# Gathering the second expert table in 2 KB half rows, into buffers of their own

## The chip, the core and the metric

The kernel runs on one NeuronCore of a Trainium2 chip. The metric is the device time of one execution in microseconds (us). The engines named are TensorE (PE, with its weight loads as PEld), VectorE (DVE), ScalarE (ACT), GpSimd (POOL), which issues the indirect transfers, and SyncE (SP), which issues all the others. Sixteen DMA engines move the data of both queues.

## The reference

One decoder layer for 1024 prompt tokens and 8 sample tokens: three mixers (a state-space scan, a convolution, attention to a memory) fed by one projection, then a PEER feed-forward, in which every token picks 128 of 16384 experts (8 heads, 16 each). All in float32.

```
x <- LN1(ALPHA * x + W_out( g_A * SSD(x) + g_B * ConformerConv(x) + g_C * MemCrossAttn(x) ))
x <- LN2(ALPHA * x + PEER(x))
# PEER for a block of tokens t (nt, 1024):
idx, gate = top-16 routing per head            # (nt, 8, 16)
u = jnp.take(u_tab, idx, axis=0)               # rows of 1024 floats
act = gelu(einsum('td,thkd->thk', t, u))
v = jnp.take(v_tab, idx, axis=0)
return einsum('thk,thkd->td', gate * act, v)
```

The first table is `peer_u`, the second `peer_v`; a row of either is 4 KB.

## The kernel before

The prompt is cut into three groups of 256, 384 and 384 tokens. For each group `main` runs the mixers as a long list of 128-column weight products on PE. The PEER layer of groups 0 and 1 (2 and 3 blocks of 128 tokens) is done by gathering rows, in the shadow of the products of the groups behind them. The PEER layer of the last group is done densely in `dense_group`: a loop over 128 chunks of 128 experts, with one product with the first table (24 matmuls, L200), a multiplication by the gate (`weigh`, L1353 on DVE), splits into high and low parts (L176, L191 on DVE) and 18 matmuls with the second table (L1385) in each.

A block goes through two stages:

- `block_u` (L447): 128 indirect transfers, each bringing one 4 KB row of the first table to each of 128 partitions (512 KB in all); DVE multiplies and sums each (L455).
- `block_v` (L480): the same with the second table. While `strips` is true the sum over experts is done on PE: for each of 32 values of m four gathers are made, and `four` (L489) multiplies them, eight matmuls together (L501; two column halves times four row strips). When the last group's mixers near their end `strips` becomes false, and the last two blocks go through `block_v2` and `second_table` on DVE instead: one scalar-tensor-tensor of 128x1024 for each gather (L544). `sample_experts` does the same for the 8 sample tokens with 64-row gathers.

All gathers are issued by POOL, one after another, at one line (L442). All rows of both tables, and the accumulators and layer-norm tiles of this part, share one pool of eight 4 KB buffers named `uv` (`UVB = 8`).

The order of the work is made at build time. Before each product `spread` (L271) adds a pace to two counters (one for each table) and takes that many steps of the tables' generators; a step is one gather. `PHASES` and `PACE` hold the paces. What has to follow a gather with a delay (`four`) is put into `late` with a number of steps (`VLAG`). A scheduler then lays the instructions of each engine in a fixed order; each engine works through its own in that order. So a step that is late holds whatever stands behind it on the same engine.

Of the kernel before, what the change touches and what calls it, by code (L numbers as in the profile page):

```python
# [8 lines left out]
F32 = mybir.dt.float32  # L9
# [9 lines left out]
P = 128  # L19
# [10 lines left out]
EPS = 1e-5  # L30
NEG = -3.0e38
TAPS = 31
UVB = 8
TICKS = (4, 6, 5)
PTICK = (1, 1, 0)

PHASES = tuple(dict(zip(("ssd", "out0", "out1", "att", "merge", "rest"), x)) for x in (
    ((0, 0),) * 6,
    ((1.7, 2), (1.8, 1.8), (1.8, 1.8), (2.2, 1.8), (1.4, 1.8), (2.4, 1.8)),
    ((1.4, 2), (1.8, 1.8), (1.8, 1.8), (2.2, 1.8), (1.4, 1.8), (2.4, 1.8))))  # L40
PACE = (1.5, 2.0), (1.0, 1.0), (2.2, 2.2)
LAG = 4
# [2 lines left out]
PRE = 6  # L45
EARLY = 30
STEP = 4
VLAG = 6
TLAG = 10
E2B = 7  # L50
BLKB = 28
# [17 lines left out]
def hybrid_layer(ctx: ExitStack, tc, I, O):  # L69
# [16 lines left out]
    def blk(n=N, dt=F32):  # L86
        t = blkp.tile([P, NW], dt, name="b")
        return t[:, :n]
# [358 lines left out]
    def block_u(g, c, idx, gate):  # L447

        x1 = pep.tile([P, D], F32, name="x1", bufs=1)
        sp.dma_start(x1, x1d[g][c])  # L450
        av = pep.tile([P, P], F32, name="av", bufs=3)
        for s in range(P):
            u = pep.tile([P, D], F32, name="uv", bufs=UVB)
            gather(u, I["peer_u"], idx[:, c, s:s + 1])
            dve.scalar_tensor_tensor(u, u, 1.0, x1, op0=OP.mult, op1=OP.mult, accum_out=av[:, s:s + 1])  # L455
            yield
        act.activation(av, av, AF.Gelu)
        dve.tensor_tensor(av, av, gate[:, c], op=OP.mult)

        def turned():  # L460

            if not strips[0]:
                tables[1].append(block_v(g, c, idx, av, None, None))
                return
            ix = blk(P)
            act.activation(ix, idx[:, c], AF.Copy)
            pt = pst()
            pe.transpose(pt[:, 0:P], av, ident)
            pe.transpose(pt[:, P:2 * P], ix, ident)
            avt = pep.tile([P, P], F32, name="avt", bufs=2)  # L470
            act.activation(avt, pt[:, 0:P], AF.Copy)
            ixt = pep.tile([P, P], I32, name="ixt", bufs=2)
            dve.tensor_copy(ixt, pt[:, P:2 * P])
            tables[1].append(block_v(g, c, idx, av, avt, ixt))

        while len(tables[1]) > 1:
            yield
        late.append([TLAG, turned])

    def block_v(g, c, idx, av, avt, ixt):  # L480


        if not strips[0]:
            yield from block_v2(g, c, idx, av)
            return
        active.append(1)
        va = []

        def four(m, vs):  # L489
            if m == 0:  # L490
                va.extend(pva() for _ in range(2))
            w = slide[m % 2]
            act.activation(w[:, :, 31], avt[:, m:P:32], AF.Copy)

            before = None
            for dh in range(2):
                for j in (3, 0, 1, 2):
                    with ExitStack() as order:
                        if before is not None:
                            order.enter_context(tc.issue_after(before))  # L500
                        before = pe.matmul(va[dh][32 * j:32 * j + 32], w[:, j, 31 - m:63 - m],  # L501
                                           vs[j][:, dh * 512:dh * 512 + 512], start=(m == 0), stop=(m == 31)).ins

        for m in range(32):
            vs = []
            for j in range(4):
                v = pep.tile([P, D], F32, name="uv", bufs=UVB)
                gather(v, I["peer_v"], ixt[:, 32 * j + m:32 * j + m + 1])
                vs.append(v)
                if j < 3:  # L510
                    yield
            late.append([VLAG, lambda m=m, vs=vs: four(m, vs)])
            yield
        done = []
        late.append([VLAG, lambda: done.append(1)])
        while not done:
            yield
        xr = pep.tile([P, D], F32, name="uv", bufs=UVB)
        sp.dma_start(xr, x1d[g][c])
        for dh in range(2):  # L520
            hs = slice(dh * 512, dh * 512 + 512)
            dve.scalar_tensor_tensor(xr[:, hs], xr[:, hs], ALPHA, va[dh], op0=OP.mult, op1=OP.add)  # L522
        active.pop()
        layer_norm2(xr, P, pep.tile([P, D], F32, name="uv", bufs=UVB))
        sp.dma_start(O[f"yp{g}"][c], xr)

    def block_v2(g, c, idx, av):

        acc = pep.tile([P, D], F32, name="uv", bufs=UVB)
        yield from second_table(P, P, idx[:, c], av, acc)  # L530
        xr = pep.tile([P, D], F32, name="uv", bufs=UVB)
        sp.dma_start(xr, x1d[g][c])
        dve.scalar_tensor_tensor(xr, xr, ALPHA, acc, op0=OP.mult, op1=OP.add)
        layer_norm2(xr, P, acc)
        sp.dma_start(O[f"yp{g}"][c], xr)
# [119 lines left out]
    def main(G):  # L655
# [41 lines left out]
        for half in range(2):  # L697
            us = []
            phase("ssd")
            for q in (2 * half, 2 * half + 1):  # L700
                us += ssd_group(G, q, G.pre if q == 0 else ssd_front(G, q))
                if ms is None:
                    ms = rp.tile([P, N], F32, name="ms")[:, :nt]
                sums(q)
                sq = [blk(nt) for _ in range(4)]
                for x, u in zip(sq, us[-4:]):
                    act.activation(x, u, AF.Square)
                squares.append((q, sq))
            if half == 0:
                acc_o = [accp.tile([P, NW], F32, name="acc")[:, :no] for _ in range(8)]  # L710
                acc = [x[:, :nt] for x in acc_o]
            if last and half == 0:
                drain()
            ops = pack(G, us, (C_NW, 8 * half), S["u"][:, 8 * half:8 * half + 8] if last else None)
            phase("out0" if half == 0 else "out1")
            if g == RIDE and half == 1:
                side.append(samples())
            for f in range(8):
                ps = out_product(G, I["wso"][half * 8 + f], ops, f, "ba", half == 1)
                if f == 0:  # L720
                    sums(4)
                    if half == 1:
                        rs = rstd_of(ms, 2048, blk(nt))
                if half == 0:
                    act.activation(acc[f], ps, AF.Copy)
                else:
                    dve.tensor_tensor(acc[f], acc[f], ps, op=OP.add)
                    dve.tensor_tensor(acc[f], acc[f], rs, op=OP.mult)
                    pg = proj(64 + f, G)
                    sg = blk(nt)  # L730
                    act.activation(sg, pg, AF.Sigmoid)
                    dve.tensor_tensor(acc[f], acc[f], sg, op=OP.mult)
                if f % 4 == 3:
                    conv_block(2 * half + f // 4)
# [783 lines left out]
```

## Time and profile before

| | |
|---|---|
| median of 3 runs | 4560.6 us (4558.73 to 4568.82) |
| profiled execution | 4556.38 us, its span 4554.6 us |
| mean granted TensorE clock | 0.936 of full speed |
| PE / DVE / ACT / POOL busy, share of the span | 86% / 72% / 38% / 35% |
| indirect transfers by POOL | 640 first table, 640 second table, 32 for the samples |

Four parts of the span matter. Until 852 us nothing is gathered. From there to about 1400 us only the first table is gathered. From 1412 to 3426 us the three strip blocks run beside the products (gaps at 1975 to 2099 and 2640 to 2762 us). From 3431 us the dense loop runs, with the gathers of the last two blocks and of the samples beside it, until 4482 us; PE's last matmul of the loop is at 4513 us. In the rows below, busy times are in us, `x` counts instructions, `L` is a line of the kernel before.

### The profile page before, as it was taken

How to read it: one execution, taken by the hardware profiler on the slowest of the kernel's cores; microseconds unless marked ns; L12 is line 12 of the kernel's file. 1: busy time of each engine (PE TensorE's matmuls, PEld its weight loads, DVE VectorE, ACT ScalarE, POOL GpSimd, SP SyncE). 2: the span in 40 equal slices, each digit the busy share in tenths (PEclk: the TensorE clock that was granted, in tenths of full speed). 3: DMA queues.
4: the chain of work that ended last, by engine and by line, in shares of the span. 5: the costliest groups of instructions: out<-in, count | busy, mean ns of one | idle time of the engine just before them, and what ended most of it. 6: DMA issues, size and time to landing. Idle time of an engine off the chain costs nothing. (4 is left out here: it accounts for less than half of the span.)

```text
span 4554.6 us, 58299 instructions
## 1 busy us (share of the span) xinstructions
PE 3933.1 (86%) x19901; PEld 3047.6 (67%) x19901; DVE 3289.7 (72%) x7235; ACT 1751.8 (38%) x3696; POOL 1593.4 (35%) x1316
## 2 busy tenths in 40 slices
PE   8998899688898788975888888888996999889996
PEld 8888788567675455553665665445664788778895
DVE  4458835869698546675766796458996899888876
ACT  5475525346432204342362332113562333333333
POOL 0000000123333554413444536534322566556631
PEclk9999999899899998987999999999997999999998
DMA  5435555556677898835878879978879999999985
GB/s 176 149 124 171 180 164 169 202 205 226 220 241 245 302 343 311 291 139 178 282 282 321 304 260 337 341 236 282 305 283 312 359 382 393 343 317 304 389 280 188
DMA packets 410043, 1199.42 MB, mean 263 GB/s; under 512 B 42465, under 2 KB 111713, under 8 KB 407569
## 3 DMA queue, kind: packets, MB, share of 16 engines
q0 software_dynamic: 186880, 679.56, 42.2%
q1 hardware_dynamic: 222864, 516.13, 32.8%
q8 instruction: 157, 2.57, 0.2%
q14 instruction: 142, 1.16, 0.1%
HBM read 1141.59 MB, written 53.93 MB: 262 GB/s over the span
## 5 line engine op out<-in xcount | busy, mean ns | idle before, releaser
L442 POOL DMA_INDIRECT uv<-in_peer_u,idx x640 | 759.0, 1186 | 1831.9 <-DVE idx L422 852.1
L200 PE MATMUL mm<-xt,wh 128*128 128x384 f32 (+1 forms) x4224 | 1045.5, 333 | 37.5 <-ACT b L923 23.9
L455 DVE SCALAR_TENSOR_TENSOR uv<-uv,x 128x1024 f32<-128x1024 f32 x640 | 775.7, 1220 | 395.0 <-DMA uv<-in_peer_u,idx 347.1
L200 PEld LDWEIGHTS mm<-xt,wh 128*128 128x128 f32 x4224 | 745.3, 193 | 100.3 <-issue 33.1
L211 PE MATMUL mm<-b,wr 128*128 128x256 f32 (+2 forms) x2304 | 724.9, 467 | 60.9 <-ACT b L739 34.1
L200 PE MATMUL mm<-xt,wl 128*128 128x384 f32 (+1 forms) x2112 | 692.0, 328 | 37.7 <-DVE wl L191 37.5
L189 ACT ACTIVATE wh<-wr 128x1024 fp32r<-128x1024 f32 x362 | 382.9, 1058 | 864.4 <-PE mm L200 327.0
L442 POOL DMA_INDIRECT uv<-in_peer_v,ixt x384 | 427.6, 1113 | 688.1 <-PE va L501 205.5
L211 PEld LDWEIGHTS mm<-b,wr 128*128 128x128 f32 x2304 | 438.4, 196 | 310.3 <-issue 45.4
L191 DVE TENSOR_TENSOR wl<-wr,wh 128x1024 fp32r<-128x1024 f32 x362 | 441.9, 1221 | 247.1 <-ACT wh L189 229.6
L442 POOL DMA_INDIRECT uv<-in_peer_v,idx x256 | 348.2, 1360 | 345.0 <-DVE uv L544 194.2
L200 PEld LDWEIGHTS mm<-xt,wl 128*128 128x128 f32 x2112 | 406.9, 193 | 57.6 <-DVE wl L191 43.4
L678 DVE SCALAR_TENSOR_TENSOR b<-raw,cc,b 128x384 f32<-128x384 f32 (+1 forms) x720 | 408.7, 569 | 9.9 <-ACT b L676 3.4
L544 DVE SCALAR_TENSOR_TENSOR uv<-uv,av 128x1024 f32<-128x1024 f32 (+1 forms) x269 | 343.5, 1280 | 12.9 <-DMA uv<-in_peer_v,idx 9.9
L501 PE MATMUL va<-uv,slide 128*32 128x512 f32 x1536 | 228.2, 714 | 133.3 <-DMA uv<-in_peer_v,ixt 133.3
L501 PEld LDWEIGHTS va<-uv,slide 128*32 128x32 f32 x1536 | 45.0, 120 | 244.4 <-DMA uv<-in_peer_v,ixt 148.6
L200 PE MATMUL st<-b,wh 128*128 128x384 f32 x784 | 205.7, 344 | 0.5 <-ACT b L832 0.5
L200 PE MATMUL tp<-b,wh 128*128 128x384 f32 x784 | 204.5, 342 | 0.0
L164 ACT ACTIVATE b<-acc 128x384 fp32r<-128x384 f32 x128 | 66.8, 525 | 348.4 <-PE va L1385 261.7
L176 DVE TENSOR_TENSOR wl<-e,wh 128x512 fp32r<-128x512 f32 x256 | 165.1, 684 | 24.2 <-ACT wh L164 22.1
L1385 PE MATMUL mm<-wh,b 128*128 128x512 f32 x512 | 165.2, 404 | 13.7 <-ACT b L164 10.1
L1385 PE MATMUL va<-wh,b 128*128 128x512 f32 x512 | 164.5, 403 | 10.9 <-DVE uv L522 10.9
(409 smaller groups left out, 6382.8 us busy)
## 6 DMA issues: line engine op xcount, KB each, us to landing
wr<-in_win SPq DMA_DIRECT2D x264, 512.0 KB
wr<-in_peer_ut SPq DMA_DIRECT2D x128, 512.0 KB
e<-in_peer_v SPq DMA_DIRECT2D x256, 256.0 KB
wr<-in_wso SPq DMA_DIRECT2D x48, 512.0 KB
wr<-in_wq SPq DMA_DIRECT2D x48, 512.0 KB
gd<-xt SPq DMA_DIRECT2D x16, 1536.0 KB
xt<-gd SPq DMA_DIRECT2D x16, 1536.0 KB
wr<-in_wmo SPq DMA_DIRECT2D x24, 512.0 KB
```

What stands on the lines that cost most here:

```text
L164: act.activation(hi, src, AF.Copy)
L176: dve.tensor_tensor(l, src, f32(h), op=OP.subtract)
L189: act.activation(wh, wr, AF.Copy)
L191: dve.tensor_tensor(wl, wr, f32(wh), op=OP.subtract)
L200: pe.matmul(ps, a[:, k], b[k0 + k], start=(i == 0), stop=(i == n - 1))
L211: pe.matmul(ps, w[:, k], xs[k], start=(k == 0), stop=(k == 7))
L442: pool.indirect_dma_start(out=dst, out_offset=None, in_=table, in_offset=bass.IndirectOffsetOnAxis(ap=idx_col, axis=0))
L455: dve.scalar_tensor_tensor(u, u, 1.0, x1, op0=OP.mult, op1=OP.mult, accum_out=av[:, s:s + 1])
L501: before = pe.matmul(va[dh][32 * j:32 * j + 32], w[:, j, 31 - m:63 - m], vs[j][:, dh * 512:dh * 512 + 512], start=(m == 0), stop=(m == 31) ...
L544: dve.scalar_tensor_tensor(acc, v, av[:, s:s + 1], acc, op0=OP.mult, op1=OP.add)
L678: dve.scalar_tensor_tensor(cv, raw[:, i:i + nt], col(C_FW, j * TAPS + i), cv, op0=OP.mult, op1=OP.add)
L1385: pe.matmul(outs[2 * tbk + dh], a[:, ts], v[:, dh * 512:dh * 512 + 512], start=(c == 0 and i == 0), stop=(c == P - 1 and i == 2))
```

## The change

Second-table rows are no longer gathered as 4 KB rows into the shared pool. The table is seen as 32768 rows of 2 KB, and two gathers, with indices 2i and 2i+1, bring the two halves. They land in eight 2 KB buffers of their own (`vv`); the shared pool `uv` keeps four 4 KB buffers. The memory is the same. A step of the second table's generator is now two half gathers; `four` is called for each half with four matmuls and waits `VLAG = 4` steps instead of 6. `block_v2` does two 128x512 instructions for each expert. The pace of the first table in group 1's `ssd` phase goes from 1.7 to 2.3. The indices are computed once for each block (`halves`, two DVE instructions), and `ms` moves from the pool `rp` to the block pool. The sample tokens still use `second_table` and `uv`.

```diff
-UVB = 8
+UVB = 4
+VB = 8
-    ((1.7, 2), (1.8, 1.8), (1.8, 1.8), (2.2, 1.8), (1.4, 1.8), (2.4, 1.8)),
+    ((2.3, 2), (1.8, 1.8), (1.8, 1.8), (2.2, 1.8), (1.4, 1.8), (2.4, 1.8)),
-VLAG = 6
+VLAG = 4
...
+        def halves(src):
+            h = pep.tile([P, 2, P], I32, name="half", bufs=2)
+            for dh in range(2):
+                dve.tensor_scalar(h[:, dh], src, 2.0, float(dh), op0=OP.mult, op1=OP.add)
+            return h
...
-            ixt = pep.tile([P, P], I32, name="ixt", bufs=2)
-            dve.tensor_copy(ixt, pt[:, P:2 * P])
-            tables[1].append(block_v(g, c, idx, av, avt, ixt))
+            tables[1].append(block_v(g, c, av, avt, halves(pt[:, P:2 * P])))
...
+    vhalf = I["peer_v"].rearrange("e (h d) -> (e h) d", h=2)
+    def half_row(idx_col):
+        v = pep.tile([P, 512], F32, name="vv", bufs=VB)
+        gather(v, vhalf, idx_col)
+        return v
...
-            for dh in range(2):
-                for j in (3, 0, 1, 2):
-                        before = pe.matmul(va[dh][32 * j:32 * j + 32], w[:, j, 31 - m:63 - m],
-                                           vs[j][:, dh * 512:dh * 512 + 512], start=(m == 0), stop=(m == 31)).ins
+            for j in (3, 0, 1, 2):
+                    before = pe.matmul(va[dh][32 * j:32 * j + 32], w[:, j, 31 - m:63 - m], vs[j],
+                                       start=(m == 0), stop=(m == 31)).ins
+        for m in range(32):
+            for dh in range(2):
-            vs = []
-            for j in range(4):
-                v = pep.tile([P, D], F32, name="uv", bufs=UVB)
-                gather(v, I["peer_v"], ixt[:, 32 * j + m:32 * j + m + 1])
-                vs.append(v)
-                if j < 3:
-                    yield
-            late.append([VLAG, lambda m=m, vs=vs: four(m, vs)])
-            yield
+                vs = []
+                for j in range(4):
+                    vs.append(half_row(ixh[:, dh, 32 * j + m:32 * j + m + 1]))
+                    if j == 1:
+                        yield
+                late.append([VLAG, lambda m=m, dh=dh, vs=vs: four(m, dh, vs)])
+                yield
...
-        yield from second_table(P, P, idx[:, c], av, acc)
+        for s in range(P):
+            for dh in range(2):
+                a = acc[:, dh * 512:dh * 512 + 512]
+                v = half_row(ixh[:, dh, s:s + 1])
+                if s == 0:
+                    dve.tensor_scalar(a, v, av[:, 0:1], None, op0=OP.mult)
+                else:
+                    dve.scalar_tensor_tensor(a, v, av[:, s:s + 1], a, op0=OP.mult, op1=OP.add)
+            yield
```

Three places show how the order moves. First POOL in the middle of the dense loop, before (`uv` filled from `peer_u` is the first table, from `peer_v` the second) and now (`vv` is a half row):

```order
L442 DMA uv_29115<-in_peer_u,idx1_16049 128x1024
L442 DMA uv_29118<-in_peer_v,idx1_16049 128x1024
L442 DMA uv_29121<-in_peer_u,idx1_16049 128x1024
L442 DMA uv_29124<-in_peer_v,idx1_16049 128x1024
L442 DMA uv_29127<-in_peer_u,idx1_16049 128x1024
L442 DMA uv_29196<-in_peer_v,idx1_16049 128x1024
```

```order
L443 DMA uv_28985<-in_peer_u,idx1_16438 128x1024
L443 DMA vv_28991<-in_peer_v,half_25912 128x512
L443 DMA vv_28997<-in_peer_v,half_25912 128x512
L443 DMA uv_28994<-in_peer_u,idx1_16438 128x1024
L443 DMA vv_29000<-in_peer_v,half_25912 128x512
L443 DMA vv_29006<-in_peer_v,half_25912 128x512
L443 DMA uv_29003<-in_peer_u,idx1_16438 128x1024
L443 DMA vv_29009<-in_peer_v,half_25912 128x512
L443 DMA vv_29081<-in_peer_v,half_25912 128x512
```

Where one gather of each table stood, there are now one and two: three instructions for the same rows.

Second, DVE over one chunk of the dense loop (`wl` and `b` are the low parts that PE waits for, `acc` is the weighed activation), before and now:

```order
L544 SCALAR_TENSOR_TENSOR uv<-uv,av 128x1024
L1353 TENSOR_TENSOR acc<-acc,xt 128x384
L191 TENSOR_TENSOR wl<-wr,wh 128x1024
L455 SCALAR_TENSOR_TENSOR uv,av<-uv,x_24769 128x1024
L544 SCALAR_TENSOR_TENSOR uv<-uv,av 128x1024
L176 TENSOR_TENSOR wl<-e_29720,wh 128x512
L176 TENSOR_TENSOR wl<-e_29724,wh 128x512
L544 SCALAR_TENSOR_TENSOR uv<-uv,av 128x1024
L455 SCALAR_TENSOR_TENSOR uv,av<-uv,x_24769 128x1024 x2
L191 TENSOR_TENSOR wl<-wr,wh 128x1024
```

```order
L549 SCALAR_TENSOR_TENSOR uv<-vv,av,uv 128x512 x2
L1373 TENSOR_TENSOR acc<-acc,xt 128x384
L192 TENSOR_TENSOR wl<-wr,wh 128x1024
L549 SCALAR_TENSOR_TENSOR uv<-vv,av,uv 128x512 x2
L456 SCALAR_TENSOR_TENSOR uv,av<-uv,x_25537 128x1024
L177 TENSOR_TENSOR wl<-e_30845,wh 128x512
L177 TENSOR_TENSOR wl<-e_30849,wh 128x512
L549 SCALAR_TENSOR_TENSOR uv<-vv,av,uv 128x512
L456 SCALAR_TENSOR_TENSOR uv,av<-uv,x_25537 128x1024
L549 SCALAR_TENSOR_TENSOR uv<-vv,av,uv 128x512 x3
L192 TENSOR_TENSOR wl<-wr,wh 128x1024
```

The rows of a gather stand between the low parts as before, at the same pace for each chunk; each second-table row is two instructions of half the width.

Third, PE at one set of the first strip block (`va` is the accumulator in PSUM, `slide` the weights), before and now:

```order
L200 MATMUL mm<-xt,wh 128x384 x2
L200 MATMUL mm<-xt,wl 128x384
L501 MATMUL va<-uv,slide_133 32x512 x8
L200 MATMUL mm<-xt,wh 128x384 x2
L200 MATMUL mm<-xt,wl 128x384
```

```order
L201 MATMUL mm<-xt,wl 128x384
L514 MATMUL va<-vv,slide_134 32x512 x4
L212 MATMUL mm<-b,wr 128x384 x8
L514 MATMUL va<-vv,slide_134 32x512 x4
L201 MATMUL mm<-xt,wh 128x384 x2
```

Eight matmuls that stood together are now two sets of four with a product between them.

## Rows read from the trace of the kernel before

**Rows 1.** The page: busy time by engine, and DMA share in 40 slices.

```profile
PE 3933.1 (86%) x19901; PEld 3047.6 (67%) x19901; DVE 3289.7 (72%) x7235; ACT 1751.8 (38%) x3696; POOL 1593.4 (35%) x1316
DMA  5435555556677898835878879978879999999985
```

**Rows 2.** Stretches (from:to, us): strip blocks 0, 1, 2, then four of the dense loop.

```profile
core 0: us, PE busy (x) PEld busy (x) DVE busy (x) ACT busy (x) POOL busy (x), PEclk, DMA share, GB/s
1412.00:1975.00 563.00, 483.23 (x2204) 311.48 (x2205) 342.37 (x825) 154.87 (x335) 259.77 (x238) 0.93 0.83 298
2099.00:2640.00 541.00, 461.31 (x2318) 322.29 (x2319) 355.05 (x623) 204.76 (x525) 266.62 (x234) 0.92 0.83 295
2762.00:3426.00 664.00, 576.34 (x2665) 350.26 (x2661) 487.18 (x1603) 234.86 (x324) 273.12 (x242) 0.95 0.82 298
...
3590.00:4072.00 482.00, 442.28 (x2120) 393.53 (x2119) 422.65 (x580) 158.28 (x266) 283.51 (x212) 0.95 1.00 364
4072.00:4222.00 150.00, 139.57 (x679) 123.01 (x677) 130.26 (x156) 55.81 (x90) 103.34 (x67) 0.99 1.02 310
4222.00:4361.00 139.00, 134.86 (x662) 121.35 (x663) 120.02 (x135) 48.73 (x80) 77.56 (x54) 0.98 0.99 366
4361.00:4486.00 125.00, 125.00 (x628) 113.10 (x628) 91.51 (x110) 45.90 (x76) 44.31 (x33) 1.00 0.80 268
```

**Rows 3.** PE's and POOL's longest waits on gathers: total us, times, longest.

```profile
PE va L501 <- DMA uv<-in_peer_v,ixt: 133.3, 45, 10.8
...
POOL uv L442 <- DVE uv L455: 783.2, 262, 38.8
POOL uv L442 <- PE va L501: 344.4, 75, 27.2
```

**Rows 4.** Chain of waits in strip block 2: start us, us, what.

```profile
2821.62 7.68 DMA uv<-in_peer_v,ixt
...
2829.35 3.47 PE va L501 x16
...
2839.11 7.56 DMA uv<-in_peer_v,ixt
```

**Rows 5.** Line L442, the gathers: ns min/median/max, first and last start us.

```profile
L442 POOL DMA_INDIRECT uv<-in_peer_u,idx x640: 932/1067/2877, 852.6 to 4019.1; - x160
L442 POOL DMA_INDIRECT uv<-in_peer_v,ixt x384: 932/938/2813, 1396.8 to 3417.4; - x192
L442 POOL DMA_INDIRECT uv<-in_peer_v,idx x256: 932/1296/4541, 3431.1 to 4482.5; - x128
L442 POOL DMA_INDIRECT uv<-in_peer_u,s_idx x16: 893/1400/7182, 4022.9 to 4114.8; - x16
```

**Rows 6.** Timeline in the dense loop, DVE and POOL: start us, us, [idle before <-releaser].

```profile
3594.74 1.21 DVE L455 SCALAR_TENSOR_TENSOR uv<-uv,x 128x1024 f32<-128x1024 f32 x1
3595.09 1.68 POOL L442 DMA_INDIRECT uv<-in_peer_u,idx  x1 [0.65 <-DVE uv L544]
...
3597.07 0.94 POOL L442 DMA_INDIRECT uv<-in_peer_v,idx  x1 [0.30 <-issue]
3597.08 0.57 DVE L1353 TENSOR_TENSOR acc<-acc,xt 128x384 f32<-128x384 f32 x1
...
4249.90 1.86 POOL L442 DMA_INDIRECT uv<-in_peer_v,idx  x1 [5.63 <-DVE uv L544]
```

**Rows 7.** DVE groups by shape: busy us, mean ns of one, idle before.

```profile
L544 DVE SCALAR_TENSOR_TENSOR uv<-uv,av 128x1024 f32<-128x1024 f32 x254 | 325.2, 1280 | 11.6 <-DMA uv<-in_peer_v,idx 9.9
L176 DVE TENSOR_TENSOR wl<-e,wh 128x512 fp32r<-128x512 f32 x256 | 165.1, 684 | 24.2 <-ACT wh L164 22.1 <-ACT b L832 2.0
L678 DVE SCALAR_TENSOR_TENSOR b<-raw,cc,b 128x384 f32<-128x384 f32 x480 | 293.7, 615 | 7.1 <-ACT b L676 1.8
```

**Rows 8.** DMA queues: packets, MB, time as a share of 16 engines.

```profile
q0 software_dynamic: 186880, 679.56, 42.2%
q1 hardware_dynamic: 222864, 516.13, 32.8%
```

More of the change, by code (lines that the diff above doesn't have):

```diff
@@ L458, in block_u @@
         dve.tensor_tensor(av, av, gate[:, c], op=OP.mult)
+        def halves(src):
[3 more added lines that the diff above has]
+            return h
         def turned():
             if not strips[0]:
-                tables[1].append(block_v(g, c, idx, av, None, None))
+                tables[1].append(block_v(g, c, av, None, halves(idx[:, c])))
                 return
@@ L478, in block_u, with block_v @@
         late.append([TLAG, turned])
-    def block_v(g, c, idx, av, avt, ixt):
+    vhalf = I["peer_v"].rearrange("e (h d) -> (e h) d", h=2)
[3 more added lines that the diff above has]
+        return v
+    def block_v(g, c, av, avt, ixh):
         if not strips[0]:
-            yield from block_v2(g, c, idx, av)
+            yield from block_v2(g, c, av, ixh)
             return
@@ L487, in block_v, with four @@
         va = []
-        def four(m, vs):
-            if m == 0:
+        def four(m, dh, vs):
+            if m + dh == 0:
                 va.extend(pva() for _ in range(2))
             w = slide[m % 2]
-            act.activation(w[:, :, 31], avt[:, m:P:32], AF.Copy)
+            if dh == 0:
+                act.activation(w[:, :, 31], avt[:, m:P:32], AF.Copy)
             before = None
-            for dh in range(2):
-                for j in (3, 0, 1, 2):
-                    with ExitStack() as order:
-                        if before is not None:
-                            order.enter_context(tc.issue_after(before))
-                        before = pe.matmul(va[dh][32 * j:32 * j + 32], w[:, j, 31 - m:63 - m],
-                                           vs[j][:, dh * 512:dh * 512 + 512], start=(m == 0), stop=(m == 31)).ins
-        for m in range(32):
-            vs = []
-            for j in range(4):
-                v = pep.tile([P, D], F32, name="uv", bufs=UVB)
-                gather(v, I["peer_v"], ixt[:, 32 * j + m:32 * j + m + 1])
-                vs.append(v)
-                if j < 3:
-                    yield
-            late.append([VLAG, lambda m=m, vs=vs: four(m, vs)])
-            yield
+            for j in (3, 0, 1, 2):
+                with ExitStack() as order:
+                    if before is not None:
+                        order.enter_context(tc.issue_after(before))
+                    before = pe.matmul(va[dh][32 * j:32 * j + 32], w[:, j, 31 - m:63 - m], vs[j],
+                                       start=(m == 0), stop=(m == 31)).ins
+        for m in range(32):
+            for dh in range(2):
+                vs = []
[5 more added lines that the diff above has]
+                yield
         done = []
@@ L525, in block_v, with block_v2 @@
         sp.dma_start(O[f"yp{g}"][c], xr)
-    def block_v2(g, c, idx, av):
+    def block_v2(g, c, av, ixh):
         acc = pep.tile([P, D], F32, name="uv", bufs=UVB)
-        yield from second_table(P, P, idx[:, c], av, acc)
+        for s in range(P):
[7 more added lines that the diff above has]
+            yield
         xr = pep.tile([P, D], F32, name="uv", bufs=UVB)
@@ L702, in main @@
                 if ms is None:
-                    ms = rp.tile([P, N], F32, name="ms")[:, :nt]
+                    ms = blk(nt)
                 sums(q)
```

## Prediction

> **What bounds the kernel now.** I read the page first, then the stretches, then the waits of PE and POOL, then the chain inside a stretch, and last the rows of the gathers. The page shows PE busy 86% of the span and no other engine above 72% [rows 1], so at first sight PE's program sets the time and POOL, at 35%, has room. The DMA digits climb to 8 and 9 in the second half. An average over stages hides what counts here, so the stretches come next [rows 2].
>
> In the three strip blocks PE is busy 86%, 85% and 87%, DVE 61% to 73%, POOL 41% to 49%, DMA 82% to 83%. The largest wait of PE is that of `four` for its second-table rows: 133.3 us in 45 pieces [rows 3]. The chain shows how that comes about [rows 4]: a gather of the second table (7.68 us until its data are used), the matmuls of `four`, and then, from 2839 us, the next such gather (7.56 us). POOL waited 344 us in all for those matmuls and 783 us for DVE's first-table rows [rows 3], since both kinds of row share eight buffers. So a strip set (four rows; 563 us / 31 = 18 us in block 0) is a loop of buffer, gather and matmul that is a little longer than PE's own work.
>
> In the dense loop DMA is at 0.99 to 1.02 from 3590 to 4361 us, DVE at 86% to 88%, PE at 92% to 97%; from 4361 us on PE is never idle [rows 2]. The cuts at 3590, 4072, 4222, 4361 and 4486 us are where DVE weighs chunks 30, 80, 96, 112 and 127, so that the order of either kernel can be counted against them.
>
> **POOL: twice the instructions for the second table.** This is the term that decides. A gather is issued one at a time; its shortest time is 932 ns for 128 rows and 893 ns for 64 rows [rows 5], so neither half the rows nor half the bytes helps much, and I take a half-row gather at the time of a whole one (the row of 64 as the lower end is 4% below). Between two gathers that wait for nothing lie 0.30 us [rows 6]. The floor is then 0.94 + 0.30 = 1.24 us for each gather. It is not reached in general: 3595.09 took 1.68 us, and at its start a DVE instruction with two SBUF inputs had 0.86 us left (3594.74 + 1.21); 3597.07 took 0.94 us, and the DVE instruction beside it began just behind it [rows 6]. A gather looks as if it waits for the two-input DVE instruction that runs when it starts. Such an instruction of 128x1024 takes 1.28 us; halves of 512 should take about 0.70 us each, between 0.615 for 384 columns and 0.684 for another operation on 512, rounded up for the in-place accumulator [rows 7]. Halves therefore hold a gather for less time.
>
> The Trainium skill speaks against such a hold ("SBUF — State Buffer", Who interferes with whom): an instruction with two SBUF inputs blocks only those GpSimd instructions that read SBUF, and writing descriptors is inferred to be spared. The pair of rows just read disagrees, so the sum follows the rows; what the page's rule would give is rival C.
>
> The mean time of a gather with its gap, from the stretches [rows 2]: 3590 to 4072 283.51/212 + 0.30 = 1.64 us; 4072 to 4222 103.34/67 + 0.30 = 1.84 us; 4222 to 4361 77.56/54 + 0.30 = 1.74 us. The upper end is a gather that is always held: 1.68 + 0.30 = 1.98 us beside both kinds of row, 1.86 + 0.30 = 2.16 us beside second-table rows alone [rows 6].
>
> Dense loop. DVE's order ties the rows to the chunks: `acc` and `wl`, for which PE waits, stand behind the rows of the chunk before, so a late gather holds DVE and then PE. What POOL must issue between the cuts, counted in the changed order, against the time of the stretch now:
>
> - chunks 30 to 80: 103 first-table gathers and 205 halves, 308 x 1.64 = 505 us against 482: +23. Floor 382 us, no loss; upper end 610 us, +128.
> - chunks 80 to 96: 1 + 55 halves + 30 for the samples, 86 x 1.84 = 158 us against 150: +8. Floor 107, no loss; upper end 86 x 2.0 = 172, +22. The samples' rows now have two free `uv` buffers at a time, which is in this upper end.
> - chunks 96 to 112, where the order packs the second table densest: 118 halves + 2, 120 gathers. Here I take 1.55 us, below 1.74, since all row instructions are halves: 186 us against 139: +47. Floor 149, +10; upper end 259, +120.
> - chunks 112 to 127: 74 halves, 115 us against 125: nothing, as PE covers it. Upper end 160, +35.
>
> Together +78 us, with +10 and +305 as the ends. Before chunk 30 the 55 gathers fit (90 us in the 159 from the first at 3431 us [rows 5]), and the 20 halves behind chunk 127 lie beside the matmuls of the last chunks.
>
> **DVE.** 256 instructions of 1.28 us become 512 of about 0.70: 256 x 0.12 = +31 us, 12 of them in chunks 30 to 80. DVE there goes from 423 to 435 us, below POOL's 505, so POOL hides it. Without that cover it would cost up to 31. The index instructions are two for each of five blocks: nothing.
>
> **DMA.** The gather queue moved 679.56 MB in 42.2 points of busy share (16.10 MB for each), the other queue, with smaller packets, 15.74 MB [rows 8]. At the latter rate the 335.5 MB of the second table cost 0.5 points more, 22 us of the span, some 9 of them in the dense loop. The slower pace there hides them; if POOL were not the bound they would show. The lower end is no gain: the bytes are the same.
>
> **Strips.** What goes: second-table rows no longer wait for a buffer that a first-table row holds, each half set is used and freed by itself, and the loop of [rows 4] becomes two loops that overlap. PE could get back up to the 133 us of [rows 3]. What comes: 31 sets of four more gathers in each block. Block 0: (238 + 124) x (259.77/238 + 0.30 = 1.39) = 503 us of 563; block 1: 358 x 1.44 = 516 of 541; block 2: 366 x 1.43 = 523 of 664 [rows 2]. POOL is then busy or in its gap 89%, 95% and 79% of the time, in order, with first-table rows queued behind second-table rows whose buffers are not free and the reverse. The next late thing behind the buffer is POOL's own queue, about as long as the loop it replaces. I take 0; the ends are -133 (no wait left) and, at the dense loop's 1.64 us, 594, 587 and 600 us: +31 +46 + 0 = +77. The waits I cannot see are those on the four `uv` buffers of the first table: DVE, not PE, meets them first, and DVE has a quarter of the time free there.
>
> The higher pace in group 1's `ssd` phase moves first-table gathers forward into a stretch where only the first table is gathered; nothing.
>
> **Sum.** 4556.4 (the profiled execution; span 4554.6) + 78 + 0 = 4634 us. The median of the runs shown is 4 us above that execution: 4638, say 4640 us.
>
> **Rivals.**
> A, the decoupling wins: the strips lose their 133 us of waits, and the dense loop costs only what POOL's floor and DVE make of it (+10 to +78). 4560 - 133 + 60 = about 4490 us. For it: the wait is the largest of PE, and POOL fits on average in all three blocks. Against it: 95% of an in-order queue in block 1. It decides if at least 85 us of the 133 go.
> B, POOL binds in both: the strips at +77 and the dense loop midway to its upper end (78 to 305: +190) give 4560 + 267 = about 4825 us. For it: the gathers of 1.68 and 1.86 us. Against it: half rows hold POOL for less.
> C, no hold by two-input instructions: POOL at 1.24 us everywhere, dense +10, strips with POOL far from full, perhaps half the 133 back, DVE's and DMA's 31 + 9 no longer hidden: 4560 + 10 + 40 - 66 = about 4545 us. (By that page's rule; the trace disagrees, as said.)
>
> **Chances.** Forecast 0.57 (own range 4585 to 4720), A 0.22, B 0.13, C 0.08. A measurement of this kernel tells 0.2%, 9 us, from no change. Faster: A and most of C, 0.27; same: 0.06, from the low edge of the forecast and the rest of C; slower: 0.67. The range leaves the lower half of A and the upper half of B out: 4490 to 4800.
>
> **What would show it.** POOL's count of gathers goes to 1952 and its busy share from 35% to over 50%. Right: in the dense loop POOL rests almost only in 0.30 us gaps, DVE's idle time is put down to half rows, the stretch from chunk 96 to 112 grows most (139 to over 170 us), and chunk 112 to the end stays. The strip blocks last within 30 us of now, with PE waiting for half rows. The gather beside half-width DVE rows is shorter than 1.86 us. Wrong: POOL still idle for a third of the dense loop, or strip blocks shorter by 30 us each.

## The result and the profile after

| | before | changed |
|---|---|---|
| median (4 runs each) | 4559.7 us (4552.5 to 4568.8) | 4909.2 us (4902.6 to 4918.7) |
| profiled execution's span | 4554.6 us | 4900.7 us |
| granted TensorE clock, mean | 0.936 | 0.915 |
| PE / DVE / POOL busy | 86% / 72% / 35% | 83% / 68% / 48% |

The changed kernel takes 1.076 times as long [1.0735, 1.0785]. The prediction was 4640 us with a range up to 4800: the sign was right, the size was not, by 269 us.

The page of the changed kernel, for [rows 1]:

```profile
PE 4054.2 (83%) x19901; PEld 3097.9 (63%) x19901; DVE 3328.5 (68%) x7498; ACT 1745.7 (36%) x3695; POOL 2333.1 (48%) x1956
DMA  5445554667678886628678678788879999988885
```

Of the 346 us of span, 121 are PE's own busy time (4054.2 against 3933.1 for the same 19901 matmuls, at the lower granted clock) and 225 its idle time. POOL is still only at 48%, which says as little as its 35% did before.

The place of the loss is read by the same cuts as [rows 2]: DVE weighs chunk 30 at 3798 us (3590 before), and chunks 80, 96, 112 and 127 at 4311, 4499, 4690 and 4821 us. The stretches of the changed kernel between them (from:to, length, busy us of each engine and its instructions, clock, DMA share, GB/s):

```profile
3798.00:4311.00 513.00, 453.11 (x2113) 397.01 (x2113) 424.71 (x666) 158.04 (x266) 402.58 (x312) 0.94 0.96 337
4311.00:4499.00 188.00, 150.95 (x688) 131.57 (x687) 133.06 (x191) 55.91 (x91) 134.33 (x88) 0.93 0.80 244
4499.00:4690.00 191.00, 154.05 (x672) 135.59 (x671) 135.10 (x201) 48.17 (x80) 149.98 (x118) 0.91 0.87 277
4690.00:4821.00 131.00, 125.60 (x618) 112.83 (x619) 101.05 (x152) 45.78 (x76) 98.66 (x77) 0.99 0.83 272
```

Against 482, 150, 139 and 125 us that is +31, +38, +52 and +6, and +11 behind the last cut: 138 us. The other 208 us are lost before chunk 30: DVE weighs chunk 0 at 3637 us (3438.5 before), so 198 of them lie ahead of the loop. They do not all lie in the strips. The 2315 products of PE (its matmuls without those of `four`) that the kernel before ran between 852 and 1400 us, where it gathered almost only the first table, last until 1450 us in the changed kernel, which has run 48 matmuls of `four` by then (first line before, second line changed):

```profile
852.00:1400.00 548.00, 469.19 (x2315) 381.09 (x2316) 444.78 (x804) 249.93 (x598) 172.78 (x142) 0.92 0.67 225
850.00:1450.00 600.00, 492.62 (x2363) 391.76 (x2364) 471.61 (x847) 250.16 (x601) 220.78 (x186) 0.89 0.68 231
```

So some 50 us are lost there, 31 of them before the first half row is gathered at 1372 us, and some 148 us in the strips. The prediction had put nothing on either.

The waits of the changed kernel, for [rows 3] (total us, times, longest):

```profile
PE va L514 <- DMA vv<-in_peer_v,half: 161.4, 62, 8.8
...
POOL uv L443 <- DVE uv L456: 541.5, 163, 35.3
POOL vv L443 <- PE va L514: 324.0, 85, 39.0
```

PE waits longer for half rows than it did for whole ones (133.3 us). The gathers, for [rows 5], and POOL in a strip (start us, us, [idle before <- releaser]):

```profile
L443 POOL DMA_INDIRECT vv<-in_peer_v,half x1280: 943/958/7475, 1372.5 to 4872.4; - x183
L443 POOL DMA_INDIRECT uv<-in_peer_u,idx x640: 934/1008/2210, 850.4 to 4300.7; - x160
```

```profile
1702.56 0.95 POOL L443 DMA_INDIRECT vv<-in_peer_v,half  x1 [0.30 <-PE va L514]
1703.82 0.95 POOL L443 DMA_INDIRECT uv<-in_peer_u,idx  x1 [0.30 <-issue]
1705.07 0.94 POOL L443 DMA_INDIRECT vv<-in_peer_v,half  x1 [0.30 <-issue]
1706.32 1.17 POOL L443 DMA_INDIRECT vv<-in_peer_v,half  x1 [0.30 <-issue]
1707.79 0.95 POOL L443 DMA_INDIRECT uv<-in_peer_u,idx  x1 [0.30 <-issue]
1709.04 1.44 POOL L443 DMA_INDIRECT vv<-in_peer_v,half  x1 [0.30 <-issue]
```

A gather of 2 KB rows costs POOL what one of 4 KB rows does (943 against 932 ns at the least), and in this piece of a strip POOL does nothing else: each gather begins 0.30 us behind the one before.

### The profile page after: what moved, and what is told of

Read it like the earlier page. It is cut to its first block, busy times and chain, and to the rows that moved or that the text cites. A ratio compares the mean times of both kernels' runs of the same rounds, so it can differ in the third digit from the quotient of the medians.

```text
span 4900.7 us, 59947 instructions
## 1 busy us (share of the span) xinstructions
PE 4054.2 (83%) x19901; PEld 3097.9 (63%) x19901; DVE 3328.5 (68%) x7498; ACT 1745.7 (36%) x3695; POOL 2333.1 (48%) x1956
## 3 DMA queue, kind: packets, MB, share of 16 engines
q0 software_dynamic: 197120, 679.60, 41.4%
## 5 line engine op out<-in xcount | busy, mean ns | idle before, releaser
L443 POOL DMA_INDIRECT vv<-in_peer_v,half x1280 | 1544.5, 1207 | 823.0 <-PE va L514 324.0
L443 POOL DMA_INDIRECT uv<-in_peer_u,idx x640 | 744.0, 1163 | 1680.7 <-DVE idx L423 879.6
L201 PE MATMUL mm<-xt,wh 128*128 128x384 f32 (+1 forms) x4224 | 1060.1, 337 | 49.3 <-ACT b L943 23.3
L201 PEld LDWEIGHTS mm<-xt,wh 128*128 128x128 f32 x4224 | 757.5, 196 | 126.1 <-issue 50.6
L212 PE MATMUL mm<-b,wr 128*128 128x256 f32 (+2 forms) x2304 | 746.5, 477 | 94.0 <-ACT b L759 52.7
L201 PE MATMUL mm<-xt,wl 128*128 128x384 f32 (+1 forms) x2112 | 703.4, 333 | 48.6 <-DVE wl L192 46.2
L549 DVE SCALAR_TENSOR_TENSOR uv<-vv,av,uv 128x512 f32<-128x512 f32 x508 | 363.0, 747 | 61.5 <-DMA vv<-in_peer_v,half 58.1
L514 PE MATMUL va<-vv,slide 128*32 128x512 f32 x1536 | 234.4, 677 | 173.0 <-DMA vv<-in_peer_v,half 161.4
L514 PEld LDWEIGHTS va<-vv,slide 128*32 128x32 f32 x1536 | 32.9, 113 | 252.7 <-DMA vv<-in_peer_v,half 189.6
L201 PE MATMUL st<-b,wl 128*128 128x384 f32 x392 | 143.0, 365 | 50.7 <-DVE wl L192 40.7
```

Source lines behind the costliest of these rows:

```text
L201: pe.matmul(ps, a[:, k], b[k0 + k], start=(i == 0), stop=(i == n - 1))
L212: pe.matmul(ps, w[:, k], xs[k], start=(k == 0), stop=(k == 7))
L443: pool.indirect_dma_start(out=dst, out_offset=None, in_=table, in_offset=bass.IndirectOffsetOnAxis(ap=idx_col, axis=0))
L549: dve.scalar_tensor_tensor(a, v, av[:, s:s + 1], a, op0=OP.mult, op1=OP.add)
```

## Experiments

Each run stands beside runs of the kernel before on the same chip, which took 4545 to 4565 us everywhere. The chips were not the same for all runs, and it will turn out that this matters. Runs that gather half rows compute the indices by `halves`; these runs, and those with nine or ten buffers, also move `ms` as the changed kernel does. The theories named in the expectations: I, the number of gathers that POOL issues sets the loss; B, the split of the buffers does in the strips; O, the shorter lag does; D, the landing of a row paces the strips; W, POOL's time is in a loop with the wait for buffers; R, POOL's rate alone; H, gathers wait for two-input DVE instructions; P, the kernel varies from chip to chip; Q, it does not.

| run (in order) | chip | us, median of 4 (half the bytes: 8) | ratio to before, 95% |
|---|---|---|---|
| two gathers per row, else as before | a | 4939.5 | 1.0802 to 1.0877 |
| the same in the strips only | a | 4806.0 | 1.0461 to 1.0590 |
| whole rows, buffers split 4 + 4 | a | 4648.7 | 1.0163 to 1.0220 |
| changed, lag 6 and pace 1.7 | a | 4877.7 | 1.0658 to 1.0720 |
| before, half the bytes in the strips | b | 4577.9 | 1.0034 to 1.0077 |
| before, half the gathers in the strips | b | 4440.2 | 0.9721 to 0.9783 |
| two gathers in the strips, nine buffers | b | 4649.6 | 1.0177 to 1.0247 |
| before, nine buffers | b | 4489.6 | 0.9837 to 0.9901 |
| changed, low parts in halves | c | 4821.1 | 1.0521 to 1.0605 |
| changed, twelve half buffers | c | 4806.8 | 1.0490 to 1.0574 |
| before, ten buffers | c | 4447.0 | 0.9714 to 0.9795 |
| changed, pace 1.7 | c | 4804.5 | 1.0480 to 1.0577 |
| changed kernel again | d | 4938.0 | 1.0809 to 1.0880 |
| pace 1.7 again | d | 4915.2 | 1.0763 to 1.0849 |
| low parts in halves again | d | 4941.9 | 1.0815 to 1.0870 |
| two gathers per row again | d | 4949.6 | 1.0831 to 1.0890 |
| two gathers in the strips again | e | 4712.3 | 1.0346 to 1.0399 |
| two gathers in the strips, nine buffers again | e | 4652.7 | 1.0217 to 1.0267 |

**Two gathers into the old buffer.**

```diff
-                gather(v, I["peer_v"], ixt[:, 32 * j + m:32 * j + m + 1])
+                for dh in range(2):
+                    gather(v[:, dh * 512:dh * 512 + 512], vhalf, ixt[:, dh, 32 * j + m:32 * j + m + 1])
```

(and the same in the dense loop's `second_table`)

> The kernel before (eight shared 4 KB buffers, sets of eight products, lag 6, pace 1.7) with one thing changed: every second-table row comes as two half-row gathers into the two halves of its one 4 KB buffer. So POOL issues 1952 gathers instead of 1312, and buffers, order and products stay. Theory I (the issue of gathers on POOL binds, in the strips as in the dense loop): strips about +200 us and dense loop with tail about +140, 4850 to 4920 us. Theory B (the strips' loss comes from the split of the buffers, only the dense loop's from POOL): strips within 30 us of before, dense loop +80 to +140, 4640 to 4720 us.

Measured 4939.5 us: the doubled gathers alone, in the old buffers, with the old products, lag and pace, cost 374 us, as much as the whole change. That is 20 us above what Theory I allowed, and the three blocks below are 225 us longer together, close to its 200. B, which had the strips within 30 us, falls. The three strip blocks of this run:

```profile
1417.00:2063.00 646.00, 510.67 (x2197) 315.63 (x2201) 342.11 (x822) 156.45 (x339) 399.56 (x362) 0.88 0.76 259
2185.00:2802.00 617.00, 488.52 (x2338) 335.10 (x2330) 359.47 (x627) 203.02 (x527) 402.85 (x353) 0.88 0.77 260
2927.00:3657.00 730.00, 599.90 (x2677) 356.76 (x2677) 490.91 (x1608) 235.18 (x324) 417.84 (x370) 0.92 0.79 274
```

Block 0: 362 gathers take 399.56 + 362 x 0.30 = 508 us with their gaps, 331 us before [rows 2]. POOL's remaining time, in which it waits for a buffer or has no gather to issue, falls from 232 to 138 us. So of 177 us more of issue 94 were taken out of the waits, and the block grew by 83 us (563 to 646). Over the three blocks the issue with its gaps grew by 532 us, from 1014 to 1546, and the blocks by 225 us: 307 us came out of the waits.

**The same in the strips alone** (the second edit left out):

> As the run with two half-row gathers into one 4 KB buffer, but in the three strip blocks alone; the second table of the dense loop is gathered in whole rows, as before. Theory I: the strips' share alone, about +200 us, 4730 to 4790 us. Theory B: 4545 to 4590 us.

4806.0 us, +241, above what Theory I allowed; PE's wait for second-table rows rose to 226.2 us in 63 pieces. The dense loop's share is the difference of the two runs, 134 us, beside the 138 us read above.

**Split buffers, whole rows.**

```diff
-                v = pep.tile([P, D], F32, name="uv", bufs=UVB)   # UVB = 8
+                v = pep.tile([P, D], F32, name="vv", bufs=VB)    # UVB = 4, VB = 4
```

> The kernel before with its eight shared 4 KB buffers split into four for the first table and four for the second; whole rows, sets of eight products, lag 6 and pace 1.7 stay, POOL issues 1312 gathers as before. Theory I: no extra gather, so within 30 us of before, 4530 to 4590 us. Theory B: a row that waits for its own kind of buffer holds the other kind behind it in POOL's order, and four buffers are one set of rows: strips +150 to +250 us, 4710 to 4810 us.

4648.7 us, +84: between the theories. With no more gathers than before the split has a price of its own, little more than half of the least that B asked for; POOL's waits for PE rise from 344 to 580 us.

```profile
POOL vv L443 <- PE va L502: 579.8, 83, 27.9
```

**The old lag and pace in the changed kernel.**

```diff
-    ((2.3, 2), (1.8, 1.8), (1.8, 1.8), (2.2, 1.8), (1.4, 1.8), (2.4, 1.8)),
+    ((1.7, 2), (1.8, 1.8), (1.8, 1.8), (2.2, 1.8), (1.4, 1.8), (2.4, 1.8)),
-VLAG = 4
+VLAG = 6
```

> The changed kernel with the lag of the products behind their gathers put back from 4 to 6 steps and the pace of the first table in group 1's ssd phase from 2.3 to 1.7. Theory O (the shorter lag puts PE's products too close behind their gathers): the wait of PE for half rows, 161 us, falls by half or more and the time to 4750 to 4830 us. Theories I and B: PE's wait only moves, 4880 to 4940 us.

4877.7 us, 2 us below what I and B allowed. O asked for 4830 or less and for a wait of PE halved from 161 us; it is 137.0 us, and O falls. Against the two-gather run on the same chip this is the effect of own half buffers and small sets alone: 62 us less. They do help; the doubled gathers cost six times that.

**Bytes or instructions.** In the strips of the kernel before, half rows (first edit), then half the number of whole rows (second):

```diff
-                gather(v, I["peer_v"], ixt[:, 32 * j + m:32 * j + m + 1])
+                gather(v[:, 0:512], vhalf, ixt[:, 0, 32 * j + m:32 * j + m + 1])
```

```diff
-                gather(v, I["peer_v"], ixt[:, 32 * j + m:32 * j + m + 1])
-                vs.append(v)
+                if j % 2 == 0:
+                    gather(v, I["peer_v"], ixt[:, 32 * j + m:32 * j + m + 1])
+                vs.append(v if j % 2 == 0 else vs[-1])
```

> The kernel before with, in the strip blocks, the first 2 KB of every second-table row gathered alone and used for both halves of the product (the second half of these rows is left out of the result). As many gathers as before (1312), half their bytes in the strips. Theory I (it is the number of gathers, not their bytes or their landing): within 30 us of before, 4530 to 4590 us. Theory D (the loop is paced by how long a row takes to land): landing of these rows falls by 2 us or more and the time by 60 to 130 us.

> The kernel before with, in the strip blocks, two of every four second-table rows gathered and each used twice (half of these rows are left out of the result); the buffers still rotate four to a set, the products stay. 192 gathers fewer. Theory I, if POOL's issue already paces the strips in the kernel before: the strips lose 60 to 130 us and PE's wait for second-table rows falls below 60 us, 4430 to 4500 us. If POOL only binds once its instructions are doubled: within 30 us of before.

Half the bytes: 4577.9 us, 27 us slower, though these rows landed 4.7 us after their issue in the median, against 6.9 us for the whole rows of the kernel with nine buffers below (the trace of the kernel before lacks a part of its landings). D falls. Half the gathers: 4440.2 us, 110 us faster, and PE's wait for these rows is all but gone (133.3 us before):

```profile
PE va L501 <- DMA uv<-in_peer_v,ixt: 8.5, 5, 4.2
```

That run brings half the bytes too, but these alone gave nothing. It also asks for a landing in half as many second-table buffers, which no run takes apart from the count, and ten buffers gain as much with every gather in place (below). So what paced the strips already in the kernel before, at 35% busy, is POOL's issue together with its waits for buffers; that the issue alone did is not shown.

**More buffers.**

```diff
-UVB = 8
-BLKB = 28
+UVB = 9
+BLKB = 26
```

> As the run with two half-row gathers into one 4 KB buffer in the strips alone (4806 us), with nine shared 4 KB buffers in place of eight (two of the 28 blocks for mixer data given up for the room). Theory W (the gathers wait for buffers, and POOL's time is in a loop with those waits): POOL's waits fall and 40 to 100 us come back, 4700 to 4765 us. Theory R (POOL's rate alone): no gain, 4790 to 4830 us.

> The kernel before with nine shared 4 KB buffers in place of eight and 26 blocks for mixer data in place of 28; 1312 whole-row gathers. The measure for the run above: under both theories what nine buffers give whole rows, 0 to 60 us less than before; if the two blocks that were given up bind, up to 30 us more.

> The kernel before with second-table rows gathered in two halves in the strips alone, once more (4806 us the first time), as the measure for the next run on the same chip. Theory I: 100 us or more above the kernel before, whatever the chip.

> The same with nine shared buffers, once more (4650 us the first time, on another chip than the run with eight). Theory W (POOL's issue stands in a loop with the wait for buffers): 80 us or more below the run with eight buffers on this chip. Theory R (POOL's issue rate alone): within 40 us of it, and the difference seen first was the chip's.

Whole rows with nine buffers: 61 us less. With halved rows the first pair seemed to give 156 us, but stood on two chips; on one chip it is 4712.3 against 4652.7, 60 us, between W and R. A ninth buffer is worth the same 60 us with either kind of row, so the doubled gathers cost about as much with nine buffers (4649.6 - 4489.6 = 160 us on chip b) as with eight (167 us on chip e, whose kernel before took 4545.3). Buffers do not buy them back.

**Twelve half buffers, and ten whole ones.**

```diff
-VB = 8        # second run: -UVB = 8
+VB = 12       #             +UVB = 10
-E2B = 7
-BLKB = 28
+E2B = 5
+BLKB = 26
```

> The changed kernel with twelve half-row buffers in place of eight (room taken from two of the 28 blocks for mixer data and two of seven 2 KB tiles of attention and scan). Theory W (the strips' loss is POOL's issue in a loop with the wait for buffers): 100 us or more come back in the strips, the dense loop, where POOL is full, stays within 20 us, 4760 to 4830 us. Theory R (POOL's rate alone, in the strips too): 4890 to 4930 us.

> The kernel before, whole rows, with ten shared 4 KB buffers in place of eight, the room taken from the same tiles as in the run with twelve half buffers. Theory W: below the 4490 us of nine buffers by 20 to 60 us, 4430 to 4470 us. If the room that was given up binds, or nine were enough: 4480 to 4520 us.

4806.8 us looks like a gain of 102, but the run beside it on that chip, whose strips are those of the changed kernel, took 4821.1. What is left is 14 us, so W's 100 us do not come. R, POOL's rate alone in the strips too, does not stand either: by the table at the end of this section the strips' loss fell from 52 to 9 us, and 17 us before them and 21 us in the first 30 chunks went the other way. Whether the room that was given up costs these is not tested. Ten whole-row buffers take 4447.0 us, 2.5% below before, and are the fastest full version found. Its strips (second-table rows wait PE only 66.0 us):

```profile
1410.00:2036.00 626.00, 528.78 (x2514) 347.66 (x2510) 412.97 (x1144) 195.82 (x451) 274.85 (x244) 0.93 0.77 282
2089.00:2568.00 479.00, 430.08 (x2252) 309.00 (x2250) 340.95 (x597) 189.13 (x475) 267.13 (x219) 0.95 0.87 320
2687.00:3273.00 586.00, 536.25 (x2481) 324.35 (x2477) 447.72 (x1501) 203.99 (x291) 272.17 (x241) 0.97 0.86 319
```

**Shorter DVE instructions, and the pace alone.**

```diff
-        dve.tensor_tensor(wl, wr, f32(wh), op=OP.subtract)
+        for q in ((slice(0, 4), slice(4, 8)) if not strips[0] else (slice(0, 8),)):
+            dve.tensor_tensor(wl[:, q], wr[:, q], f32(wh[:, q]), op=OP.subtract)
```

(the pace run has the first of the two edits of the lag run)

> The changed kernel with, from the dense loop on, each weight's low part (a DVE subtraction of 128x1024, 1.22 us) made in two instructions of 128x512. Theory H (a gather waits for the two-input DVE instruction that runs at its start, and POOL is the bound of the dense loop): the gathers' mean there falls from 1.33 to below 1.28 us and the time by 10 to 35 us, 4875 to 4900 us. Without the hold: POOL's mean stays, DVE does some 13 us more beside it, 4900 to 4925 us.

> The changed kernel with the pace of the first table in group 1's ssd phase put back from 2.3 to 1.7 alone; the lag stays at 4. If the pace made the 32 us by which lag 6 and pace 1.7 together were faster: 4870 to 4885 us. If the lag did: 4900 to 4920 us.

4821.1 and 4804.5 us, and both gains were false. In the first run DVE, POOL and the rest stand in the changed kernel's order until the dense loop, and yet it reached that loop 97 us earlier. Hence the next four runs, on one chip:

> The changed kernel once more, unaltered, on the same chip as the three runs that follow. The run with the low parts in halves (4821 us) has the same order of instructions as the changed kernel on every engine until the dense loop, and yet was 97 us ahead at that point. Theory P (the changed kernel itself varies, by the chip or by where a load of it lands): it comes back at 4800 to 4860 us. Theory Q (the difference belongs to the program): 4890 to 4925 us.

> The changed kernel with pace 1.7 alone, once more (4805 us the first time). If the pace costs what it seemed to: some 100 us below the changed kernel on this chip. If Theory P holds: within 30 us of it.

> The changed kernel with the low parts in halves from the dense loop on, once more (4821 us the first time). Theory Q: some 90 us below the changed kernel on this chip. Theory P, with the order equal until the dense loop: within 20 us of it.

> The kernel before with every second-table row gathered in two halves into its one 4 KB buffer, once more (4940 us the first time), for the difference to the changed kernel on one chip. If the rest of the change (own buffers, sets of four, lag, pace) gives nothing: within 30 us of the changed kernel. If it gives what the run with lag 6 and pace 1.7 seemed to show: 40 us or more above it. Theory P would show here as well, as a time 50 us or more from the first one.

The changed kernel took 4938.0 us here, above what either theory named, and the low parts in halves 4941.9: within 4 us of it, as P asks, and 121 us above the very same program on chip c. Q falls, and P had named too small a spread. The difference goes with the chip, or with the session, for each chip was used in one. From chunk 30 to 127 a gather took 781.71/588 = 1.33 us in the mean beside the shorter DVE instructions and 777.61/588 = 1.32 us in the changed kernel, where H asked for less than 1.28; H is not shown. The pace is worth 23 us in the total; the two intervals overlap. The two-gather run differs from the changed kernel by 12 us with overlapping intervals: everything else in the change (own buffers, small sets, lag, pace) nets to nothing that shows. Its times on chips a and d are 10 us apart.

**Where the runs lose.** The products of PE without those of `four` stand in nearly the same order in all these kernels, so a profiled execution can be set against that of the kernel before at the same product, and from chunk 0 on at the same `weigh`. Us lost in each stretch of the kernel before:

| run | chip | 852 to 1400 us | to chunk 0 (strips) | chunks 0 to 30 | 30 to 127 | behind |
|---|---|---|---|---|---|---|
| changed, first result | not on record | 50 | 148 | 9 | 127 | 11 |
| changed again | d | 55 | 161 | 13 | 140 | 12 |
| pace 1.7 again | d | 2 | 184 | 8 | 148 | 11 |
| pace 1.7 | c | 4 | 87 | 7 | 132 | 10 |
| low parts in halves again | d | 60 | 166 | 10 | 157 | 11 |
| low parts in halves | c | 48 | 52 | 9 | 143 | 11 |
| twelve half buffers | c | 65 | 9 | 30 | 134 | 9 |
| two gathers per row | a | 0 | 229 | 4 | 133 | 0 |
| two gathers per row again | d | 8 | 236 | 6 | 143 | 0 |
| two gathers, strips only | a | 7 | 234 | -1 | 0 | -1 |
| two gathers, strips only again | e | 15 | 146 | 0 | -6 | 0 |

## Why the prediction was wrong

**Strips: "I take 0; the ends are -133 (...) and [...] +77".** This step failed. The changed kernel lost 148 us in the strips, and the doubled gathers in the old buffers lose 229. Its count of POOL was right: 503 us foretold for block 0, 508 measured in the two-gather run. The inference was not. It compared POOL's issue time with the length of the block ("89%, 95% and 79%") and took what POOL waits as room. But POOL's other time in the strips (232 us of 563 in block 0) goes for the most part into waits for buffers, which PE and DVE free only after the rows have landed and been used, and only a part of it gave way (138 us of 646 are left). In block 0 before (first two lines) and in the two-gather run (last two), the wait for DVE's rows shrank, the wait for PE's matmuls stayed:

```profile
POOL uv L442 <- DVE uv L455: 105.9, 38, 8.2
POOL uv L442 <- PE va L501: 93.8, 19, 27.2
POOL uv L442 <- PE va L509: 88.2, 16, 24.0
POOL uv L442 <- DVE uv L455: 35.8, 12, 6.1
```

Issue and waits follow each other in the one queue. Of 532 us more issue in the three blocks 307 came out of the waits and 225 were added to the time; the half-count run shows the same the other way, 192 gathers fewer, with the buffers that they wait for, gave 110 us. The upper end (+77) made the same error, as it let the waits go to zero before time was lost.

**Dense loop: +78, measured +138.** The place was right, and so were the prices: with its gap a gather took 402.58/312 + 0.30 = 1.59 us (1.64 foretold), 1.83 (1.84), 1.57 (1.55) and 1.58 us. Right too was that chunks 96 to 112 grow most, +52 for +47. What was missing are POOL's rests, taken as none: 513 - 312 x 1.59 = 17 us, 27 us where the samples' rows have two free buffers, 6 us behind that, and 11 us behind the last cut, put at nothing. The doubled gathers alone explain it (134 us in the difference of the two-gather runs).

**DVE and DMA: hidden.** The half row of DVE, for [rows 7], and the queues, for [rows 8]:

```profile
L549 DVE SCALAR_TENSOR_TENSOR uv<-vv,av,uv 128x512 f32<-128x512 f32 x508 | 363.0, 747 | 61.5 <-DMA vv<-in_peer_v,half 58.1 <-issue 2.4 <-DVE uv L549 0.7
```

```profile
q0 software_dynamic: 197120, 679.60, 41.4%
q1 hardware_dynamic: 222864, 516.13, 31.2%
```

A half row took 0.747 us for 0.70, and DVE was busy 425 of 513 us from chunk 30 to 80, so the cover was there. DMA's share of that stretch fell from 1.00 [rows 2] to 0.96. The gather queue's own time rose by more than foretold, from 42.2% of 4554.6 to 41.4% of 4900.7 us: 107 us and not 22, beside POOL's slower pace.

**Index instructions and pace: nothing.** The prediction put the pace at nothing since its stretch gathers the first table alone, and gave no price for that; in that stretch it is not nothing. On chip d, with the pace as the only difference, the products of the kernel before from 852 to 1400 us took these times (first line pace 1.7, second line 2.3, with 52 matmuls of `four`):

```profile
852.00:1402.00 550.00, 470.59 (x2316) 381.56 (x2317) 442.49 (x799) 250.03 (x598) 166.96 (x140) 0.92 0.66 219
852.00:1455.00 603.00, 494.20 (x2368) 392.90 (x2372) 472.14 (x847) 250.37 (x601) 222.51 (x187) 0.89 0.68 230
```

The 53 us come back in part in the strips (161 us lost there, for 184 with pace 1.7), so the total shows 23 us, not told from zero.

**The rivals.** A fell: the decoupling is real (62 us less with own half buffers and small sets), but PE's wait for second-table rows rose from 133 to 161 us where A asked that 85 us of it go. B named the mechanism, POOL binding in both, at 4825 us; it put +190 on the dense loop and +77 on the strips, and it is 138 and 148, with 50 us of the pace that no rival had. C's time, 4545 us, fell. The rule behind it is not settled. The Trainium skill, "SBUF — State Buffer", Who interferes with whom, says that an instruction with two SBUF inputs holds up only those GpSimd instructions that read SBUF. Gathers of 0.95 and of 1.44 us still stand side by side in the rows above, but shorter DVE instructions made neither the mean gather (1.33 us for 1.32) nor the kernel shorter.

**What would show it.** 1952 gathers: yes. Busy share over 50%: 48%. POOL in the dense loop at rest almost only in its gaps: yes, but for 60 of 1023 us. DVE's idle time there put down to half rows: in part, 56.5 us, and 75.2 us to first-table rows. Chunks 96 to 112 grow most: yes. Chunk 112 to the end unchanged: +17. Strips within 30 us: no.

## What to carry to other kernels

The busy share of an in-order queue is not its room: of what a queue waits in a loop with its own consumers only a part gives way when its instructions take longer (307 of 532 us here), so extra instructions are not free as long as they fit into the stretch. Before a transfer is cut into smaller ones, halve the number of instructions in one stage with the work left out: here that showed in one run (-110 us) that the count of gathers, with the buffers that they wait for, paced the stage, and half the bytes in another (+27) that they did not. Two more whole buffers in the shared pool, with room taken from other tiles, gave 117 us; splitting the same room into two pools cost 84. A change of pace is priced in the stretch where it acts, even if the total hardly shows it. And a variant is compared with its parent on the same chip.

## What was not expected of the hardware

Kernels with halved rows differed from chip to chip by up to 2.5% (the program with the low parts in halves 4821 and 4942 us, two gathers in the strips 4712 and 4806 us), the kernel before did not (4545 to 4565 us on all five). By the table above the difference lies nearly all in the strips: 52 and 166 us, 146 and 234 us. The gathers' own times agree (1.34 and 1.33 us in the mean from chunk 30 to 127 on chips c and d).

The traces differ in one more thing, which bears on how they are read: records are missing. On chips b, c and e the traces hold at least 99.9% of the records of the gathers' landings. On chips a and d those with halved rows hold 61% to 69%, the trace of the first result 67%, that of the kernel before 89%. Where they are missing, DVE has idle time that the profile puts down to nothing ("issue"): in the slower of the two traces of the program with the low parts in halves 229.5 us in 85 pieces, in the faster there is no such row. Of the changed kernel on chip d:

```profile
DVE wl L192 <- issue: 84.9, 33, 9.5
DVE uv L456 <- issue: 61.9, 29, 6.4
DVE b L353 <- issue: 32.5, 9, 18.3
```

A wait whose releaser left no record would look the same, so these rows name no cause. Whether the lost records and the lost time have one cause stays open. So does how much of the first result's 350 us is the chip's: its chip is not on record, by its records it is like a and d, and the changed kernel itself was not run on chip c. If it stands to its variant there as it does on chip d, it would take some 4820 us there (an estimate). The strips' loss, 52 us in that variant, would then lie inside the prediction's ends, but with the dense loop and the pace the time would still be outside the range.
